# Attention steps of four heads, a free accumulator, and matmuls on constants while the first loads run

## The chip, the cores and the metric

The kernel runs on one core of a Trainium2 chip. The metric is the device time in microseconds, the median of several runs. TensorE (PE) does the matmuls, VectorE (DVE) and ScalarE (ACT) work on their operands and results, GpSimd (POOL) makes masks, and SyncE (SP) issues most of the loads.

## The reference, cut to what matters

Three mixers over a sequence of 256 tokens of 2048 features, each with its input and output projections in full precision:

- `hybrid_layer`: a convolution branch (gated input, 31 taps, layer norm) beside attention with 16 heads of 64 features, two shared keys and values, a window of 128 and a sink per head. Its output is projected, added to the input and normed.
- `_dsa_mixer`: an index of 16 heads of 64 features scores the earlier tokens and keeps the best 64 for each query (`k_top = min(256, S // 4)`); attention with 16 heads of 128 features in four groups of four, each group with one key and one value head, runs over the kept ones.
- `_stick_breaking_mixer`: 16 heads of 128 features with their own keys and values; the weights come from sums of log-sigmoids.

The second and third are each followed by a norm and a gate: `x = x + (p[i] @ w_ple[i]) * sigmoid(x @ w_ple_gate[i])`.

## The kernel before

**Projections.** Every large product is made of matmuls on operands split into two parts (`hi`, `lo`): three products stand for one in full precision. `gemm` (L315) keeps activations stationary and streams 512 weight columns (L324 to L326); `gemm_T` (L329) keeps 128 weight columns stationary: per k-tile and feature tile of 128 columns, one matmul of 512 columns on both parts of the activation (L336), one of 256 columns for the low part of the weight (L338). `granules` (L291) walks the weight in pieces of one, two or four k-tiles. `fetch` (L268) loads a piece, casts its high part on ACT (L277) and subtracts on DVE (L278), two pieces ahead; `plan` fixes the order of the weights.

**PSUM.** `acc` has two tiles of two banks for the projections, `aux` four banks that `bank` (L215) hands out for everything else: scores, transposes, weighed values. `gemm_T` takes one `acc` tile for each two feature tiles, so `gv0` (gate and value together, four feature tiles) takes both. `total` (L341) adds the two halves of a result: an ACT copy, then a DVE addition.

**Side work.** `Side` (L153) holds lanes of generators. After each weight piece `pump` lets every lane take a step, lanes "a" and "b" in turn. The scheduler then orders instructions by program order and by when it takes them to be ready; each engine runs its own queue in order.

- `conv` (L502) in lane "conv": 31 multiply-adds on DVE for each of eight channel tiles, three taps a step.
- `soften` (L534) for two heads: scores into a bank each, the row minimum of the negated scores on DVE, then a step with the exponentials and the scaling on ACT (or DVE), then a step with three transposes a head into a bank each and their copies. `attn1` (L624) calls it for head i of both key groups, one on partitions 0 to 63 and the other on 64 to 127, so its score matmuls use half the rows (L547, L548) and its weighing half the columns (L593, L594); these are in full precision. A record of the profile is one pass; a full-precision matmul has two.
- `index()` (L918): 16 heads, two a step (L926, L927), each with a relu on ACT (L929) that frees its bank and two DVE multiply-adds.
- `attn2` (L985): scores of 128 queries in full precision (L543) and of the others in three split matmuls (L545); weighing by `weigh_split` (L596), three split matmuls (L602) and a full-precision one of 128 columns (L603) a head.
- `attn3` (L1038): a step per head with three split matmuls (L1044) and a full-precision one (L1048) into a bank that stays in use until its exponential; then two steps of sums by triangular ones (L1062, L1063), then `weigh_split`.

The transposes of `kvT` into `v1` (L731) stand straight behind the projection `kv`.

## Time and profile before

| | |
|---|---|
| median of 3 runs | 1449.77 us (1449.68 to 1450.47) |
| the profiled execution | 1450.28 us, its span 1448.6 us |
| PE busy | 1432.4 us, 8076 matmul records |
| DVE, ACT busy | 1032.3 us, 802.9 us |
| HBM read | 262.53 MB, 183 GB/s |

The page gives each engine's busy time, then the span in 40 slices. A row of the timeline is a run of like instructions on one engine: start, time from the first start to the last end, engine, line, operation, shapes, count, and in brackets the idle time before it with what ended it. Matmuls overlap in these rows (their ends are modelled); what one costs is read from start to start.

### The profile page before, as it was taken

What the parts mean: (1) busy time and instruction counts of PE and PEld (TensorE: products, weight loads), DVE (VectorE), ACT (ScalarE), POOL (GpSimd) and SP (SyncE); (2) the same over time, 40 slices, a digit from 0 to 9 for tenths busy, and PEclk for the clock granted to TensorE, in tenths of its full rate; (3) what the DMA queues carried; (4) which work ended last, traced back from release to release, by engine and by line L of the source; (5) the groups of instructions that cost most, each with busy time, mean ns of one, the idle gap of its engine ahead of it and who ended that gap; (6) DMA issues with size and microseconds to landing.
All of it is one profiled execution on the core that took longest, in us unless ns stands there. A gap on an engine that the chain in (4) does not pass through costs nothing.

```text
span 1448.6 us, 21304 instructions
## 1 busy us (share of the span) xinstructions
PE 1432.4 (99%) x8076; PEld 1240.1 (86%) x8076; DVE 1032.3 (71%) x1588; ACT 802.9 (55%) x1199; POOL 23.1 (2%) x51
## 2 busy tenths in 40 slices
PE   7999999999999999999999999999999999999998
PEld 6888888888997888888898898888888888889888
DVE  6999989998679966766758655655555555575754
ACT  6445778475545556646544545655655656554442
POOL 0000000000000000000000000100100001000000
PEclk9999999999999999999999999999999999999999
DMA  9765445556375655454764555555555555586462
GB/s 300 273 202 176 153 139 173 186 186 230 92 238 160 204 162 173 148 186 152 260 201 148 184 178 187 162 176 188 169 179 175 175 176 167 185 266 218 128 219 75
DMA packets 79798, 266.01 MB, mean 184 GB/s; under 512 B 9408, under 2 KB 10048, under 8 KB 79696
## 3 DMA queue, kind: packets, MB, share of 16 engines
q1 hardware_dynamic: 79632, 264.63, 56.5%
q8 instruction: 63, 1.03, 0.3%
q14 instruction: 39, 0.32, 0.1%
q0 software_dynamic: 64, 0.03, 0.0%
HBM read 262.53 MB, written 2.10 MB: 183 GB/s over the span
## 4 chain that ended last, share of the span: by engine, by line
PE 93%; DVE 4%; DMA 1%; issue 1%; ACT 1%; DVEq 0%; SPq 0%
PE acc L336 31%; PE acc L338 15%; PE acc L324 14%; PE acc L326 14%; PE acc L325 14%; DVE wlo L278 1%; PE o L602 1%; PE pt L383 1%; PE pT L578 1%; PE o L603 0%; DVE u L448 0%; DVE u L509 0%; PE z L1044 0%; PE z L1062 0%; DMA raw<-in_w_in_a 0%
## 5 line engine op out<-in xcount | busy, mean ns | idle before, releaser
L278 DVE TENSOR_TENSOR wlo<-raw,whi 128x1024 fp32r<-128x1024 f32 (+3 forms) x475 | 563.2, 1190 | 309.0 <-ACT whi L277 304.6
L277 ACT CAST whi<-raw 128x1024 fp32r<-128x1024 f32 (+3 forms) x475 | 485.2, 1025 | 489.3 <-PE acc L336 220.4
L336 PE MATMUL acc<-u,whi 128*128 128x512 f32 x2016 | 637.2, 399 | 7.3 <-DVE u L377 5.6
L338 PEld LDWEIGHTS acc<-u,wlo 128*128 128x128 f32 x2016 | 377.0, 188 | 87.7
L338 PE MATMUL acc<-u,wlo 128*128 128x256 f32 x2016 | 394.9, 279 | 0.0
L324 PE MATMUL acc<-whi,u 128*128 128x512 f32 (+3 forms) x1004 | 359.0, 358 | 0.0
L325 PE MATMUL acc<-wlo,u 128*128 128x512 f32 (+3 forms) x1004 | 355.9, 354 | 0.8 <-DVE wlo L278 0.8
L326 PE MATMUL acc<-whi,u 128*128 128x512 f32 (+3 forms) x1004 | 355.6, 354 | 0.0
L336 PEld LDWEIGHTS acc<-u,whi 128*128 128x128 f32 x2016 | 309.3, 189 | 14.2 <-ACT whi L277 5.6
L326 PEld LDWEIGHTS acc<-whi,u 128*128 128x128 f32 x1004 | 189.7, 189 | 25.4 <-DVE u L377 0.4
L324 PEld LDWEIGHTS acc<-whi,u 128*128 128x128 f32 x1004 | 189.8, 189 | 25.0 <-issue 1.7
L325 PEld LDWEIGHTS acc<-wlo,u 128*128 128x128 f32 x1004 | 189.9, 189 | 24.3 <-DVE wlo L278 1.2
L509 DVE SCALAR_TENSOR_TENSOR u<-u,convw,u 128x255 f32<-128x255 f32 (+19 forms) x240 | 109.2, 465 | 3.9
L351 DVE TENSOR_TENSOR h<-acc,h 128x512 f32<-128x512 f32 x51 | 34.8, 684 | 4.8 <-ACT h L345 4.8
L376 ACT CAST u<-h 128x512 fp32r<-128x512 f32 (+1 forms) x32 | 18.0, 566 | 25.3 <-DVE h L615 17.5
L466 DVE TENSOR_TENSOR u<-u,h 128x1024 f32<-128x1024 f32 x24 | 28.5, 1219 | 3.4 <-DMA h<-in_ln_g 3.3
L377 DVE TENSOR_TENSOR u<-h,u 128x512 fp32r<-128x512 f32 (+1 forms) x32 | 19.7, 622 | 14.4 <-ACT u L376 14.1
L1034 POOL TENSOR_SCALAR_AFFINE_SELECT h<-h 128x256 f32<-128x256 f32 x32 | 18.1, 564 | 743.8 <-DVE h L1054 715.7
L558 ACT ACTIVATE u<-u,negm 128x128 f32<-128x128 f32 x64 | 28.4, 445 | 2.7 <-DVE negm L550 2.6
L345 ACT ACTIVATE h<-acc 128x512 f32<-128x512 f32 x42 | 24.9, 593 | 5.5 <-PE acc L338 4.0
L802 DVE TENSOR_TENSOR h<-h,u 128x512 f32<-128x512 f32 (+1 forms) x20 | 10.8, 582 | 20.8 <-ACT h L801 20.8
L277 ACT CAST u<-raw 128x1024 fp32r<-128x1024 f32 (+1 forms) x17 | 17.3, 1015 | 14.2 <-DMA raw<-in_w_ple 7.4
(197 smaller groups left out, 962.8 us busy)
## 6 DMA issues: line engine op xcount, KB each, us to landing
raw<-in_w_in_a SPq DMA_DIRECT2D x80, 512.0 KB, 3.6
raw<-in_w_in SPq DMA_DIRECT2D x76, 512.0 KB, 3.4
raw<-in_w_gate SPq DMA_DIRECT2D x64, 512.0 KB, 3.6
raw<-in_w_kv_b SPq DMA_DIRECT2D x64, 512.0 KB, 3.4
raw<-in_w_q_b SPq DMA_DIRECT2D x64, 512.0 KB, 3.3
raw<-in_w_out SPq DMA_DIRECT2D x32, 512.0 KB, 3.4
raw<-in_w_out_a SPq DMA_DIRECT2D x32, 512.0 KB, 4.3
raw<-in_w_out_b SPq DMA_DIRECT2D x32, 512.0 KB, 4.4
```

Of the source, the lines that this page charges most:

```text
L277: nc.scalar.copy(hi, raw)
L278: return hi, lo, nc.vector.tensor_tensor(lo, raw, hi.bitcast(F32), ALU.subtract)
L324: nc.tensor.matmul(o, ah, wh, start=first, stop=False)
L325: nc.tensor.matmul(o, ah, wl, start=False, stop=False)
L326: nc.tensor.matmul(o, al, wh, start=False, stop=last)
L336: nc.tensor.matmul(ps[f // 2][:, f % 2], wh[:, f * P:(f + 1) * P], both, start=first, stop=False)
L338: nc.tensor.matmul(ps[f // 2][:, f % 2, 0, :], wl[:, f * P:(f + 1) * P], ah, start=False, stop=last)
L345: nc.scalar.activation(t, ps[:, :, 1, :], AF.Copy, scale=scale)
L351: nc.vector.tensor_tensor(out_, ps[:, :, 0, :], t, ALU.add)
L466: nc.vector.tensor_tensor(self.z[c], self.z[c], r.unsqueeze(1).broadcast_to([P, 2, 512]), op)
L509: nc.vector.scalar_tensor_tensor(o[:, d:], h[:, :S - d], w, o[:, d:], ALU.mult, ALU.add)
L558: nc.scalar.activation(sc[:, i, cs], sc[:, i, cs], AF.Exp, bias=negm[:, i, tt:tt + 1], scale=-1.0, accum_out=den[:, i, tt:tt + 1],)
```

## The change

`WARM` matmuls on `ones_mean` into a bank that nobody reads stand right behind the constants. `gemm_T` takes one `acc` tile for its first two feature tiles and a bank of `aux` for each further one (only `gv0` has such), and `total` takes these as a list. The transposes into `v1` stand behind the projection of `q0`. `soften` takes four heads: four banks of scores, then per two heads the minima, the exponentials, and after twelve transposes the copies, each a step of its own; split heads issue all full-precision scores ahead of all split ones. `attn1` and `attn2` use it in one lane, "heads", which steps at every pump. `index()` issues four heads' matmuls at once. The second attention's values are split for both token tiles (`both_split`), its probabilities for the late queries too, and `weigh_shared` multiplies the late queries of two heads in one matmul of 256 columns, three in all, in place of two full-precision ones. `weigh_split`, now for the third attention alone, and `attn3` issue the split matmuls of both heads ahead of the full-precision ones.

```diff
+WARM = 9
...
+    idle = bank("idle")
+    for i in range(WARM):
+        nc.tensor.matmul(idle[:, 0:P], ones_mean, ones_mean, start=True, stop=True)
...
         nf = _cols(STREAMS[stream][key][0]) // P
-        ps = [acc.tile([P, 2, 2, S], F32, tag="acc", name=uid("acc")) for _ in range(nf // 2)]
+        two = acc.tile([P, 2, 2, S], F32, tag="acc", name=uid("acc"))
+        ps = [two[:, f] for f in range(2)]
+        ps += [bank("acc").rearrange("p (h s) -> p h s", h=2) for _ in range(2, nf)]
         for kt, first, last, wh, wl in granules(stream, key, events):
-            both, ah = act.both(kt), act(kt, slice(0, S))[0]
+            pair, ah = act.both(kt), act(kt, slice(0, S))[0]
             for f in range(nf):
-                nc.tensor.matmul(ps[f // 2][:, f % 2], wh[:, f * P:(f + 1) * P], both, start=first, stop=False)
+                nc.tensor.matmul(ps[f], wh[:, f * P:(f + 1) * P], pair, start=first, stop=False)
             for f in range(nf):
-                nc.tensor.matmul(ps[f // 2][:, f % 2, 0, :], wl[:, f * P:(f + 1) * P], ah, start=False, stop=last)
-        return ps
+                nc.tensor.matmul(ps[f][:, 0, :], wl[:, f * P:(f + 1) * P], ah, start=False, stop=last)
+        return [two, ps[2:]][:nf // 2]
...
+        if isinstance(ps, list):
+            for f, p in enumerate(ps):
+                nc.scalar.activation(t[:, f, :], p[:, 1, :], AF.Identity, bias=bias1[:, bias + f:bias + f + 1])
+                nc.vector.tensor_tensor(out_[:, f, :], p[:, 0, :], t[:, f, :], ALU.add)
+            return out_
...
     def soften(heads, mask, scale):
+        twos = (heads[:2], heads[2:])
+        split = heads[0][2] is None
+        sc = [unit((P, 2, 384)) for _ in twos]
...
+        ps = [bank("s", 384) for _ in heads]
+        for p, (q, k, h) in zip(ps, heads):
+            if split:
+                nc.tensor.matmul(p[:, 0:128], q.raw, k.raw, start=True, stop=False)
+            else:
+                nc.tensor.matmul(p[:, 0:128], q[:, 0:128], k[:, 0:128], start=True, stop=True)
+                nc.tensor.matmul(p[:, 128:384], q[:, 128:256], k, start=True, stop=True)
+        if split:
+            for p, (q, k, h) in zip(ps, heads):
                 for m, (a, b) in enumerate(((q.hi, k.hi), (q.hi, k.lo), (q.lo, k.hi))):
+                    nc.tensor.matmul(p[:, 128:384], a, b, start=False, stop=m == 2)
+        for j, two in enumerate(twos):
+            for i, (q, k, h) in enumerate(two):
+                for tt, cs in enumerate(QUERIES):
+                    nc.vector.tensor_tensor_reduce(
+                        sc[j][:, i, cs], ps[2 * j + i][:, cs], mask[:, cs], -scale,
+                        3e38 if split else nsink[:, h:h + 1], ALU.add, ALU.min, negm[j][:, i, tt:tt + 1],
+                    )
+            yield
...
+        pts = [bank("pT", 384) for _ in heads]
+        for i, pt in enumerate(pts):
+            for b in range(3):
+                nc.tensor.transpose(pt[:, b * P:(b + 1) * P], sc[i // 2][:, i % 2, b * P:(b + 1) * P], ident)
+        out_ = []
+        for j in range(2):
+            if split:
+                late, early = short((P, 2, 2, P), F32R), []
+                for i, pt in enumerate(pts[2 * j:2 * j + 2]):
+                    wp = short((P, 2, S), F32R)
+                    nc.scalar.copy(wp[:, 0, :], pt[:, 0:S])
+                    nc.vector.tensor_tensor(wp[:, 1, :], pt[:, 0:S], wp[:, 0, :].bitcast(F32), ALU.subtract)
+                    hi, lo = late[:, 0, i, :], late[:, 1, i, :]
+                    nc.scalar.copy(hi, pt[:, S:384])
+                    nc.vector.tensor_tensor(lo, pt[:, S:384], hi.bitcast(F32), ALU.subtract)
+                    early.append(wp)
+                out_.append((early, late))
             else:
+                pb = [short() for _ in range(2)]
+                for i in range(2):
+                    nc.scalar.copy(pb[i], pts[2 * j + i])
                 out_.append(pb)
+            if j == 0:
+                yield
...
         vv, vl = v
         for i, (h, (wp, late)) in enumerate(zip(heads, probs)):
-            cs = slice(h * P, (h + 1) * P)
-            for m, (a, b) in enumerate(((0, 0), (0, 1), (1, 0))):
-                nc.tensor.matmul(po[:, i, :], vv[:, a, cs], wp[:, b, :], start=i == 0 and m == 0, stop=False)
-            nc.tensor.matmul(po[:, i, P:S], vl[:, cs], late, start=False, stop=i == 1)
+            for m, (a, b) in enumerate(PARTS):
+                nc.tensor.matmul(
+                    po[:, i, :], vv[:, a, h * P:(h + 1) * P], wp[:, b, :], start=i == 0 and m == 0, stop=False
+                )
+        for i, (h, (wp, late)) in enumerate(zip(heads, probs)):
+            nc.tensor.matmul(po[:, i, P:S], vl[:, h * P:(h + 1) * P], late, start=False, stop=i == 1)
+    def weigh_shared(po, v, probs, h):
+        early, late = probs
+        for i, wp in enumerate(early):
+            for m, (a, b) in enumerate(PARTS):
+                nc.tensor.matmul(
+                    po[:, i, :], v[0][:, a, h * P:(h + 1) * P], wp[:, b, :], start=i == 0 and m == 0, stop=False
+                )
+        for m, (a, b) in enumerate(PARTS):
+            nc.tensor.matmul(po[:, :, P:S], v[1][:, a, h * P:(h + 1) * P], late[:, b], start=False, stop=m == 2)
...
+    def both_split(ps):
+        out_ = [unit((P, 2, 512), F32R) for _ in range(2)]
+        for vv, p in zip(out_, ps):
+            nc.scalar.copy(vv[:, 0, :], p)
+            nc.vector.tensor_tensor(vv[:, 1, :], p, vv[:, 0, :].bitcast(F32), ALU.subtract)
+        return out_
...
-    def attn1(i):
+    def attn1(j, f):
         rows = (slice(0, 64), slice(64, 128))
-        gen = soften([(qT[i // 4][r, i % 4, :], kvT[r, 0, :], 8 * j + i) for j, r in enumerate(rows)], mask1, 0.125)
+        ii = (2 * f, 2 * f + 1)
+        gen = soften(
+            [(qT[j][r, i, :], kvT[r, 0, :], 8 * g + 4 * j + i) for i in ii for g, r in enumerate(rows)], mask1, 0.125
+        )
         for probs in gen:
             yield
-        while i // 4 not in sagT:
-            yield
-        po = bank("o1", S)
-        for r, p in zip(rows, probs):
-            weigh(po[r, :], [v1[:, tt, r] for tt in range(2)], p)
-        gate_into(yact, 8 + i, 1, po.rearrange("p (k s) -> p k s", k=1), sagT[i // 4][:, i % 4:i % 4 + 1, :])
+        while j not in sagT:
+            yield
+        po = [bank("o1", S) for _ in ii]
+        for o, two in zip(po, probs):
+            for r, p in zip(rows, two):
+                weigh(o[r, :], [v1[:, tt, r] for tt in range(2)], p)
+        for o, i in zip(po, ii):
+            gate_into(yact, 8 + 4 * j + i, 1, o.rearrange("p (k s) -> p k s", k=1), sagT[j][:, i:i + 1, :])
         yield
...
     glu(3)
     projected("kv", kvT)
-    pt = transposes([kvT[:, 1, tt * P:(tt + 1) * P] for tt in range(2)])
-    nc.scalar.copy(v1, pt[:, :S].rearrange("p (k s) -> p k s", k=2))
     for j in range(2):
         for f, h in enumerate("xy"):
             projected(f"q{j}{h}", qT[j][:, 2 * f:2 * f + 2, :])
-        for i in range(4 * j, 4 * j + 4):
-            side.add(attn1(i), 1, "ab"[i % 2])
+        if j == 0:
+            pt = transposes([kvT[:, 1, tt * P:(tt + 1) * P] for tt in range(2)])
+            nc.scalar.copy(v1, pt[:, :S].rearrange("p (k s) -> p k s", k=2))
+        for f in range(2):
+            side.add(attn1(j, f), 1, "heads")
         sag = unit((P, 4, S))
         for f, h in enumerate("xy"):
             projected(f"ag{j}{h}", sag[:, 2 * f:2 * f + 2, :], AF.Silu)
...
-    side.drain("a")
-    side.drain("b")
+    side.drain("heads")
...
+        for h0 in range(0, 16, 4):
+            ps = [bank("ix", 384) for _ in range(4)]
+            for h, p in enumerate(ps, h0):
+                rows = slice(64 * (h % 2), 64 * (h % 2) + 64)
+                qh = qiT[h // 2 // 3][:, h // 2 % 3, :]
+                nc.tensor.matmul(p[:, 0:128], qh[rows, 0:128], kiT[rows, 0:128], start=True, stop=True)
+                nc.tensor.matmul(p[:, 128:384], qh[rows, 128:256], kiT[rows, :], start=True, stop=True)
+            for h, p in enumerate(ps, h0):
...
+                if h % 2:
+                    yield
...
     kT2 = Turned("k", slice(0, S))
-    v2 = split_values(gemm("w_in_a_2", "v", xact))
+    v2 = both_split(gemm("w_in_a_2", "v", xact))
     yact = Act()
     SCALE2 = 128.0 ** -0.5
-    def attn2(qT2, c, heads, sgT):
+    def attn2(qT2, c, sgT):
         while not selected:
             yield
-        gen = soften([(qT2.head(h), kT2.head(c), None) for h in heads], bias2, SCALE2)
+        gen = soften([(qT2.head(h), kT2.head(c), None) for h in range(4)], bias2, SCALE2)
         for probs in gen:
             yield
         while c not in sgT:
             yield
-        po = bank("o2").rearrange("p (k s) -> p k s", k=2)
-        weigh_split(po, v2, probs, (c, c))
-        gate_into(yact, 4 * c + heads[0], 2, po, sgT[c][:, heads[0]:heads[0] + 2, :])
-        yield
+        po = [bank("o2").rearrange("p (k s) -> p k s", k=2) for _ in range(2)]
+        for o, two in zip(po, probs):
+            weigh_shared(o, v2, two, c)
+        for j, o in enumerate(po):
+            gate_into(yact, 4 * c + 2 * j, 2, o, sgT[c][:, 2 * j:2 * j + 2, :])
+            yield
...
-        side.add(attn2(qT2, c, (0, 1), sgT), 1, "a")
-        side.add(attn2(qT2, c, (2, 3), sgT), 1, "b")
+        side.add(attn2(qT2, c, sgT), 1, "heads")
...
     def attn3(q, k, c, heads, v3, sgT):
         zs, ws = [], []
-        for h in heads:
-            zz = bank("z", 384)
+        banks = [bank("z", 384) for _ in heads]
+        for zz, h in zip(banks, heads):
             blocks = zz.rearrange("p (b q) -> p b q", b=3)
             for i, (ks, qs) in enumerate(((k.hi, q.hi), (k.hi, q.lo), (k.lo, q.hi))):
                 nc.tensor.matmul(
                     blocks[:, 0:3:2, :], ks[:, h, 0:128], qs[:, h, :].rearrange("p (b q) -> p b q", b=2),
                     start=i == 0, stop=False,
                 )
+        for zz, h in zip(banks, heads):
             nc.tensor.matmul(zz[:, 128:256], k.late[:, h, :], q.late[:, h, :], start=False, stop=True)
+        for zz in banks:
             e, sp = short(), short()
             sh, sl = short(dt=F32R), short(dt=F32R)
             nc.scalar.activation(e, zz, AF.Abs)
```

## Rows read from the trace of the kernel before

**Rows 1.** The page: busy times, and the granted clock in 40 slices.

```profile
PE 1432.4 (99%) x8076; PEld 1240.1 (86%) x8076; DVE 1032.3 (71%) x1588; ACT 802.9 (55%) x1199; POOL 23.1 (2%) x51
...
PEclk9999999999999999999999999999999999999999
```

**Rows 2.** Who waited for whom, PE: us in total, times, longest us.

```profile
PE acc L336 <- DVE u L377: 5.6, 1, 5.6
...
PE acc L325 <- DVE wlo L278: 0.8, 1, 0.8
```

**Rows 3.** Timeline, all engines, from 0 to 34 us.

```profile
5.59 2.04 PE L336 MATMUL acc<-u,whi 128*128 128x512 f32 x4 [5.59 <-DVE u L377]
...
10.80 1.09 PE L336 MATMUL acc<-u,whi 128*128 128x512 f32 x4
...
26.47 0.69 DVE L377 TENSOR_TENSOR u<-h,u 128x512 fp32r<-128x512 f32 x1 [1.98 <-ACT u L376]
...
27.64 1.09 PE L336 MATMUL acc<-u,whi 128*128 128x512 f32 x4
...
29.97 0.63 PE L338 MATMUL acc<-u,wlo 128*128 128x256 f32 x4
...
32.27 0.73 PE L336 MATMUL acc<-u,whi 128*128 128x512 f32 x2 [1.67 <-DVE h L351]
```

**Rows 4.** A stretch: length, busy us of each engine, clock, DMA share, GB/s.

```profile
16.00:20.00 4.00, 4.00 (x25) 3.51 (x24) 2.19 (x5) 2.53 (x5) 0.00 (x0) 1.00 0.99 319
```

**Rows 5.** Timeline of PE from 108 to 121 us.

```profile
115.48 0.41 PE L383 MATMUL pt<-ident,h 128*128 128x128 f32 x2 [1.65 <-DVE h L351]
```

**Rows 6.** Timeline of PE from 136.5 to 140 us, a score group of the first attention.

```profile
136.87 0.63 PE L336 MATMUL acc<-u,whi 128*128 128x512 f32 x2
137.34 0.39 PE L338 MATMUL acc<-u,wlo 128*128 128x256 f32 x2
...
139.09 0.40 PE L338 MATMUL acc<-u,wlo 128*128 128x256 f32 x2
```

**Rows 7.** Timeline of PE from 148 to 170 us, a weighing group of it.

```profile
163.09 0.39 PE L338 MATMUL acc<-u,wlo 128*128 128x256 f32 x2
...
164.79 0.39 PE L338 MATMUL acc<-u,wlo 128*128 128x256 f32 x2
```

**Rows 8.** The chain that ended last: start us, us, what.

```profile
151.00 0.66 PE pT L578 x6
```

**Rows 9.** Timeline of PE at two index groups.

```profile
443.24 0.39 PE L338 MATMUL acc<-u,wlo 128*128 128x256 f32 x2
...
444.76 0.39 PE L325 MATMUL acc<-wlo,u 128*128 128x512 f32 x1
...
455.01 0.50 PE L926 MATMUL ix<-kiT,u 64*128 64x128 f32 x4
```

**Rows 10.** Timeline of ACT from 430 to 470 us, the relu of head 11.

```profile
456.31 0.49 ACT L929 ACTIVATE h<-ix 128x384 f32<-128x384 f32 x1 [2.81 <-DVE h L877]
```

**Rows 11.** Timeline of PE from 498 to 532 us, second attention, scores and weighing.

```profile
503.07 0.38 PE L543 MATMUL s<-h,h 128*128 128x128 f32 x2
...
503.64 0.39 PE L543 MATMUL s<-h,h 128*128 128x128 f32 x2
...
522.99 0.39 PE L338 MATMUL acc<-u,wlo 128*128 128x256 f32 x2
...
524.83 0.40 PE L338 MATMUL acc<-u,wlo 128*128 128x256 f32 x2
```

**Rows 12.** Line L543: what its engine waited for, us, times.

```profile
  ACT h L974: 1.8, 4
```

**Rows 13.** A stretch with the convolution, columns as in rows 4.

```profile
80.00:120.00 40.00, 38.35 (x221) 33.20 (x220) 39.58 (x71) 17.57 (x22) 0.00 (x0) 1.00 0.60 194
```

**Rows 14.** Who waited for whom, ACT, from 120 to 280 us.

```profile
ACT whi L277 <- PE acc L336: 32.8, 24, 1.9
```

**Rows 15.** Line L1044: what its engine waited for, us, times.

```profile
  DVE u L1028: 1.2, 4
```

More of the change, by code (lines that the diff above doesn't have):

```diff
@@ L348, in total @@
                 nc.scalar.activation(t[:, f, :], ps[:, f, 1, :], AF.Identity, bias=bias1[:, bias + f:bias + f + 1])
-        out_ = t if out_ is None else out_
         if scale == 1.0:
@@ L564, in soften @@
-        if heads[0][2] is not None:
-            nc.vector.tensor_tensor(den, den, es, ALU.add)
-        nc.vector.reciprocal(den, den)
-        for i in range(n):
-            for tt, cs in enumerate(QUERIES):
-                if h is None:
-                    nc.vector.tensor_scalar(sc[:, i, cs], sc[:, i, cs], den[:, i, tt:tt + 1], None, ALU.mult)
-                else:
-                    nc.scalar.activation(sc[:, i, cs], sc[:, i, cs], AF.Copy, scale=den[:, i, tt:tt + 1])
-        yield
-        out_ = []
@@ L575, in soften @@
-        for i in range(n):
-            pt = bank("pT", 384)
-            for b in range(3):
-                nc.tensor.transpose(pt[:, b * P:(b + 1) * P], sc[:, i, b * P:(b + 1) * P], ident)
-            if h is None:
-                wp, late = short((P, 2, S), F32R), short((P, P))
-                nc.scalar.copy(wp[:, 0, :], pt[:, 0:S])
-                nc.vector.tensor_tensor(wp[:, 1, :], pt[:, 0:S], wp[:, 0, :].bitcast(F32), ALU.subtract)
-                nc.scalar.copy(late, pt[:, S:384])
-                out_.append((wp, late))
-            else:
-                pb = short()
-                nc.scalar.copy(pb, pt)
+        twos = (heads[:2], heads[2:])
@@ new lines, in soften @@
+        for j, two in enumerate(twos):
+            es = small.tile([P, 2, 2], F32, tag="es", name=uid("es"))
+            for i, (q, k, h) in enumerate(two):
+                for tt, cs in enumerate(QUERIES):
+                    nc.scalar.activation(
+                        sc[j][:, i, cs], sc[j][:, i, cs], AF.Exp, bias=negm[j][:, i, tt:tt + 1], scale=-1.0,
+                        accum_out=den[j][:, i, tt:tt + 1],
+                    )
+                if not split:
+                    nc.scalar.activation(es[:, i, :], negm[j][:, i, :], AF.Exp, bias=sink[:, h:h + 1])
+            if not split:
+                nc.vector.tensor_tensor(den[j], den[j], es, ALU.add)
+            nc.vector.reciprocal(den[j], den[j])
+            for i in range(2):
+                for tt, cs in enumerate(QUERIES):
+                    if split:
+                        nc.vector.tensor_scalar(sc[j][:, i, cs], sc[j][:, i, cs], den[j][:, i, tt:tt + 1], None, ALU.mult)
+                    else:
+                        nc.scalar.activation(sc[j][:, i, cs], sc[j][:, i, cs], AF.Copy, scale=den[j][:, i, tt:tt + 1])
+            yield
```

57 lines of the change are left out of this document (15 added, 42 removed).

## The prediction

> **What bounds the kernel now.** I read the page's busy times first, then PE's waits, then PE's timeline at the places that the change touches. PE is busy 99% of the span at full clock from its first slices on [rows 1]. Busy alone proves little, since matmuls overlap in the records; what proves it are the waits. In 1448.6 us PE waits 5.6 us for its first operands and 0.8 us for a split weight; the other two waits of note are 1.67 and 1.65 us [rows 2, 3, 5]. Everything else is start following start: two k-tiles of gv0, eight L336 of 512 columns and eight L338 of 256, take 2.80 us [rows 3], so a k-tile with two feature tiles takes 0.70: a pair of L336 0.47 [rows 6], a pair of L338 the other 0.235. So the time is the sum of what PE is given to do plus those few holes, and an edit counts by what it takes out of PE's stream or out of a hole, as long as ACT and DVE, which split each weight (L277, L278), keep up. In the stretch with the convolution DVE is busy 39.58 of 40 us [rows 13], so there this "as long as" is the question.
>
> My unit is the insertion: from the L338 pair before a foreign group to the next L338 pair, less the plain 0.70 us.
>
> **The change part by part.**
>
> *Warm-up.* Nine full-precision matmuls on ones_mean run while the first loads fly. Before, PE starts at 5.59 and its first two k-tiles of gv0 take until 10.80, that is 5.21 us; two later ones take 2.80 (27.64 to 29.97, plus the last four L338, 0.47) [rows 3]. At most 2.4 us are there to be had. But gv0 is fed by loads: the split of the last x pair ends at 27.16 and its k-tiles start at 27.64, so the end of gv0 can move by 0.48 at most unless that load comes sooner, and the DMA engines are at 0.99 [rows 3, 4]. Between 0 and 0.48 I take **0.25 us**. [...]
>
> *gv0's accumulators.* Two of four feature tiles go to the four-bank pool, so g1 finds a free accumulator. Before, gv0's last matmul ends at 30.44 and g1 starts at 32.27, released by the total at L351 [rows 3]. Gone: **1.83 us**. What is late next is g1's own split weight; the wait names the total alone, so the weight was there before it. Bounds 1.2 to 1.9, the lower if DVE, which then has 1.8 us less in hand, makes one late later.
>
> *Values of the first attention.* The two transposes of kvT that waited 1.65 us for a total [rows 5] move behind q0's two projections, 32 k-tiles or 22 us later; the wait goes whole, and the copy v1 is needed only by the first weighing, later still. **1.65 us**, bounds 1.2 to 1.65.
>
> *First attention, scores and weighing in fours.* A score group of two heads: L338 at 137.34, next L338 at 139.09, less 0.70: 1.05 us [rows 6]. What would it cost inside a longer group? A pass of 128 full-precision columns takes 0.11 us (six transposes in 0.66 us [rows 8]); a pair needs 128 and 256 columns in two passes each (its four records of a line are two heads times two passes, the heads side by side on 64 rows each), twice 0.11 and twice 0.22: 0.66 us. The 0.39 left over is entering and leaving the 64-row form. Eight groups become four: 4 x 0.39 = **1.56 us**. Weighing: 164.79 - 163.09 - 0.70 = 1.00 [rows 7], same columns, so 4 x 0.34 = **1.36 us**. Each lies between half of this (if entry costs again within the group, for which no row exists) and all. The probability transposes have no such overhead: 0.66 for six is six times 0.11, so twelve in a row gain nothing.
>
> *Index in fours.* The same form: 443.24 to 444.76 less an L338 pair (0.235) and one L324 (0.23) is 1.05 [rows 9], eight groups to four, 1.56 us. But four banks are the whole pool, and the last group of four takes its banks when head 11's relu is done. That relu runs 456.31 to 456.80 while PE was at heads 12 and 13 already at 455.01 [rows 9, 10]: 1.8 us of waiting where none was, since before it needed heads 8 and 9 alone. Between +1.56 and -1.8 (both ends of rows) I take **0**, because the stretch ends in PE's 0.8 us wait for a split weight [rows 2], which says that DVE sets its end.
>
> *Second attention.* Grouping full-precision before split scores: one head takes 0.57 us (503.07 to 503.64) [rows 11], and 2 x 0.11 plus 3 x 0.118 is 0.57, so a switch between the kinds costs next to nothing in this form. The first one waits for its operand, 1.8 us over the four chunks [rows 12]; the new order wants the same operand first. **0.2 us**, bounds 0 to 1.8. Shared values: two heads were 524.83 - 522.99 - 0.70 = 1.14 us [rows 11]; six split matmuls plus three shared ones of 256 columns are 9 x 0.118 = 1.06. Eight times 0.08: **0.65 us**, bounds 0.3 (if the output in two strips of 128 were slower) to 0.9. Added beside it are one more 512-column split of v, and per two heads two short ACT copies and DVE subtractions of 128 columns; they lie on DVE and ACT, busy 71% and 55% of the span [rows 1], and cost nothing while probabilities are ready a step ahead; if not, each is at most one such operation late.
>
> *Third attention.* Four z matmuls wait for the low half of q or k, 1.2 us together [rows 15]; grouping two heads lets PE take another head's ready matmul first. **0.4 us** of 0 to 1.2. The reordered weighing gains nothing by the switch price above: **0**.
>
> Sum: 0.25 + 1.83 + 1.65 + 1.56 + 1.36 + 0 + 0.2 + 0.65 + 0.4 = 7.9 us. The profiled execution took 1450.28 us (1448.6 of span); by it the new time is 1442.4. The median of the runs is 0.5 us lower, so **1441.9 us**. All lower ends together (with 0.8 + 0.7 for the two fours and -1.8 for the index) give 2.4 us or 1447.4; all upper ends, 12.4 us or 1437.4.
>
> **The rivals.**
>
> *ACT and DVE set the pace (0.13).* With DVE at 39.58 of 40 us, a PE that runs 5 us earlier through the convolution may only wait more for split weights, and everything saved before the index is given back; left are 0.2 + 0.65 + 0.4 plus a part of the rest, some 2 us: **1447.8**. For it: that DVE row. Against it: from 120 to 280 us ACT's cast of the next weight waits 24 times for PE to let a buffer go, 32.8 us in all [rows 14], so the helpers are held back by PE there and not the other way.
>
> *Banks become the bound (0.08, slower).* Steps of four ask for all four banks at once: 4 score and 4 transposing steps in the first attention, the same in the second, 4 in the index, 20 in all. Before, a step needed two, and its readers had a step more of time. If each waits for the last reader, PE loses what DVE or ACT is behind. The break-even is 7.9 / 20 = 0.4 us each; at 0.6 us, a third of the 1.8 us that the index row gives, the loss is 12 us: **1453.9**. Against it: between scores and transposes lie four steps, and only the index reuses its banks two steps later.
>
> [...] Worked from rows: a fall to the lower level at each of the 20 steps for one k-tile pair of the kind that took 5.21 instead of 2.80 us would cost some 48 us, near **1490**. This case's trace speaks against it, the clock row shows full speed across both holes of 1.7 us [rows 1, 3, 5]; I give it 0.01.
>
> *The warm-up pays in full (0.04).* If the loads come sooner once PE frees its buffers sooner, all 2.4 us of the slow opening return, 2.15 more than I count: **1439.7**. The DMA share of 0.99 speaks against it.
>
> [...]
>
> That the change does not do what it says is possible for the warm-up alone (the clock may rise no sooner); that costs 0.25.
>
> **How the numbers follow.** Forecast 0.74 at 1441.9 (own range 1437.4 to 1447.4), pace 0.13 at 1447.8, banks 0.08, clock 0.01, full warm-up 0.04. The range 1436.9 to 1447.4 takes in the bounds of the unknown costs and the full warm-up's likeliest time. A measurement here can tell about 0.2% or 2.9 us from no change, so faster means under 1446.9: 0.74 + 0.04 and a little of the pace case, 0.79; same 0.12; slower 0.09.
>
> **What would show it.** Right: no wait of PE for L351 in the first 130 us; half as many 64-row score groups, each near 1.7 us for four heads; z and weighing groups as priced. Wrong: new rows of PE waiting for ACT or DVE at a score, index or transposing group (banks), or for the split weight L278 between 40 and 300 us (pace); a full clock well before 10 us with gv0 ending near 28 (warm-up).

## The result and the profile after

The changed kernel takes 1441.94 us (median of 6 runs, 1440.59 to 1443.18) against 1449.72 us (1448.77 to 1453.32): a ratio of 0.9942, 95% interval 0.993 to 0.9955, so 6.5 to 10.1 us less. The forecast was 1441.9 us. The profiled execution took 1443.18 us, its span 1441.5; before it was 1448.6, so the two traces differ by 7.1 us, and it is these that the terms are measured in.

From the page of the changed kernel:

```profile
span 1441.5 us, 21329 instructions
PE 1431.0 (99%) x8086; PEld 1245.7 (86%) x8086; DVE 1033.7 (72%) x1606; ACT 798.4 (55%) x1195; POOL 24.3 (2%) x51
```

What PE waits for in it (us in total, times, longest):

```profile
PE acc L330 <- DVE wlo L283: 1.5, 2, 0.9
PE acc L346 <- DVE u L392: 1.2, 3, 0.8
PE idle L229 <- DVE halfpi L910: 1.2, 1, 1.2
```

The kernel is bound as before [rows 1]: PE is busy 99% of the span. The two waits for a total (L351 before, now L366) are gone [rows 3, 5]. One wait has doubled, that of L330 for a split weight (0.8 us before [rows 2]). L346 waits for a split of x three times instead of once, though for less time in all, since the warm-up now fills most of the wait for the first one. L346 and L348 are the old L336 and L338, L329 to L331 the old L324 to L326.

PE's timeline of the changed kernel shows the terms one by one: the warm-up and gv0, gv0's end, the transposes of kvT, a group of scores, a group of weighing, the index's two waits, and the shared values.

```profile
1.15 4.21 PE L229 MATMUL idle<-ones_mean 128*128 128x128 f32 x18 [1.15 <-DVE halfpi L910]
6.19 2.04 PE L346 MATMUL acc<-u,whi 128*128 128x512 f32 x4 [0.83 <-DVE u L392]
...
11.10 1.08 PE L346 MATMUL acc<-u,whi 128*128 128x512 f32 x4
...
14.21 1.20 PE L346 MATMUL acc<-u,whi 128*128 128x512 f32 x4 [0.17 <-DVE u L392]
...
17.45 1.20 PE L346 MATMUL acc<-u,whi 128*128 128x512 f32 x4 [0.16 <-DVE u L392]
...
31.11 0.64 PE L348 MATMUL acc<-u,wlo 128*128 128x256 f32 x4
31.58 0.63 PE L346 MATMUL acc<-u,whi 128*128 128x512 f32 x2
...
132.06 0.40 PE L348 MATMUL acc<-u,wlo 128*128 128x256 f32 x2
132.29 0.38 PE L398 MATMUL pt<-ident,h 128*128 128x128 f32 x2
...
132.97 0.40 PE L348 MATMUL acc<-u,wlo 128*128 128x256 f32 x2
...
135.06 0.40 PE L348 MATMUL acc<-u,wlo 128*128 128x256 f32 x2
135.39 0.50 PE L561 MATMUL s<-h,u 64*128 64x128 f32 x4
135.71 0.61 PE L562 MATMUL s<-h,u 64*128 64x256 f32 x4
136.15 0.49 PE L561 MATMUL s<-h,u 64*128 64x128 f32 x4
136.37 0.70 PE L562 MATMUL s<-h,u 64*128 64x256 f32 x4
...
137.58 0.40 PE L348 MATMUL acc<-u,wlo 128*128 128x256 f32 x2
...
160.51 0.39 PE L348 MATMUL acc<-u,wlo 128*128 128x256 f32 x2
...
162.90 0.40 PE L348 MATMUL acc<-u,wlo 128*128 128x256 f32 x2
...
447.72 0.50 PE L330 MATMUL acc<-wlo,u 128*128 128x512 f32 x1 [0.65 <-DVE wlo L283]
453.50 0.50 PE L330 MATMUL acc<-wlo,u 128*128 128x512 f32 x1 [0.90 <-DVE wlo L283]
...
518.12 0.40 PE L348 MATMUL acc<-u,wlo 128*128 128x256 f32 x2
...
520.99 0.39 PE L348 MATMUL acc<-u,wlo 128*128 128x256 f32 x2
```

Read as the prediction read it, from L348 to the next L348 less 0.70: the transposes cost 0.21 us, four heads' scores 1.82 (two cost 1.05 before [rows 6]), four heads' weighing 1.69 (two cost 1.00 [rows 7]), two pairs' values 2.17 (one cost 1.14 [rows 11]). g1's first L346 stands at 31.58, right behind gv0's last L348.

Over all groups of each kind, in us of PE's time saved:

| term | forecast | the two traces | where it is read |
|---|---|---|---|
| warm-up | 0.25 | -1.14 | gv0 ends at 31.58, before at 30.44 |
| gv0's accumulators | 1.83 | 1.83 | g1 starts at once |
| transposes of kvT | 1.65 | 1.84 | 2.06 before, 0.21 to 0.23 after |
| first attention, scores | 1.56 | 1.22 | 8 x 1.05 to 1.06, then 4 x 1.80 to 1.83 |
| first attention, weighing | 1.36 | 1.24 | 8 x 0.99 to 1.02, then 4 x 1.70 |
| index | 0 | 0 | 9.5 in both, waits for split weights included |
| second attention, scores | 0.2 | 0.79 | 10.54, then 9.75, waits included |
| second attention, values | 0.65 | 0.70 | 8 x 1.17, then 4 x 2.16 |
| third attention, z | 0.4 | 0.5 | 10.26, then 9.76 |
| sum | 7.9 | 7.0 | |

A new wait for a split weight at 73.6 us costs 0.4. It stands in all six traces with a warm-up (this one and those of experiments 1 to 4 and 7), and at 0 to 0.2 us in the eight without, so it goes with the warm-up. The projections' 7248 matmul records are the same in both traces and come in the same order; followed along their starts, the saving is -1.14 us at gv0's end, 2.3 ahead of the first attention, 4.8 behind it, 4.75 behind the index, 6.3 behind the second attention and 7.1 at the end. So the 0.5 us that the table and the wait leave open are 0.1 behind gv0, 0.1 in the second attention and 0.2 in the third (0.7 there in all); the rest is rounding.

### The profile page after: what moved, and what is told of

The parts are those of the page before. It is cut to its first block, busy times and chain, and to the rows that moved or that the text cites. A ratio compares the mean times of both kernels' runs of the same rounds, so it can differ in the third digit from the quotient of the medians.

```text
span 1441.5 us, 21329 instructions
## 1 busy us (share of the span) xinstructions
PE 1431.0 (99%) x8086; PEld 1245.7 (86%) x8086; DVE 1033.7 (72%) x1606; ACT 798.4 (55%) x1195; POOL 24.3 (2%) x51
## 4 chain that ended last, share of the span: by engine, by line
PE 96%; DVE 2%; ACT 1%; DMA 0%; issue 0%; DVEq 0%
PE acc L346 32%; PE acc L348 16%; PE acc L329 14%; PE acc L331 14%; PE acc L330 14%; PE pt L398 1%; PE pT L598 1%; DVE u L463 0%; PE z L1125 0%; PE z L1105 0%; PE o L633 0%; PE o L644 0%; DVE wlo L283 0%; PE s L566 0%; PE o L623 0%; DMA h<-in_xT 0%
## 5 line engine op out<-in xcount | busy, mean ns | idle before, releaser
L346 PE MATMUL acc<-u,whi 128*128 128x512 f32 x2016 | 636.3, 398 | 1.2 <-DVE u L392 1.2
L348 PEld LDWEIGHTS acc<-u,wlo 128*128 128x128 f32 x2016 | 377.4, 188 | 87.9 <-DVE wlo L283 0.5
L348 PE MATMUL acc<-u,wlo 128*128 128x256 f32 x2016 | 395.0, 279 | 0.1
L329 PE MATMUL acc<-whi,u 128*128 128x512 f32 (+3 forms) x1004 | 358.3, 357 | 0.0
L330 PE MATMUL acc<-wlo,u 128*128 128x512 f32 (+3 forms) x1004 | 356.5, 355 | 1.5 <-DVE wlo L283 1.5
L331 PE MATMUL acc<-whi,u 128*128 128x512 f32 (+3 forms) x1004 | 355.9, 355 | 0.0
L346 PEld LDWEIGHTS acc<-u,whi 128*128 128x128 f32 x2016 | 309.7, 190 | 6.2 <-issue 2.5
L330 PEld LDWEIGHTS acc<-wlo,u 128*128 128x128 f32 x1004 | 190.1, 189 | 25.8 <-DVE wlo L283 2.3
L331 PEld LDWEIGHTS acc<-whi,u 128*128 128x128 f32 x1004 | 189.9, 189 | 25.1 <-DVE u L392 0.4
L329 PEld LDWEIGHTS acc<-whi,u 128*128 128x128 f32 x1004 | 189.9, 189 | 24.3 <-issue 0.7
L524 DVE SCALAR_TENSOR_TENSOR u<-u,convw,u 128x255 f32<-128x255 f32 (+22 forms) x240 | 108.4, 471 | 3.1
L366 DVE TENSOR_TENSOR h<-acc,h 128x512 f32<-128x512 f32 x50 | 34.3, 686 | 2.2 <-ACT h L364 2.2
L392 DVE TENSOR_TENSOR u<-h,u 128x512 fp32r<-128x512 f32 (+1 forms) x32 | 19.9, 621 | 10.0 <-ACT u L391 9.7
```

The lines of the kernel that those rows point to most:

```text
L329: nc.tensor.matmul(o, ah, wh, start=first, stop=False)
L330: nc.tensor.matmul(o, ah, wl, start=False, stop=False)
L331: nc.tensor.matmul(o, al, wh, start=False, stop=last)
L346: nc.tensor.matmul(ps[f], wh[:, f * P:(f + 1) * P], pair, start=first, stop=False)
L348: nc.tensor.matmul(ps[f][:, 0, :], wl[:, f * P:(f + 1) * P], ah, start=False, stop=last)
L366: nc.vector.tensor_tensor(out_, ps[:, :, 0, :], t, ALU.add)
```

## The experiments

Each kernel was timed beside the kernel before on the same chip (four chips in all; there the kernel before took 1450.88 to 1451.81 us by its medians). So ratios compare across groups, microseconds only within one. The interval of a ratio is about 0.0013 to either side, 1.9 us.

**1. The warm-up taken out, made longer, and the other edits undone or moved (one chip).**

```
-WARM = 9
+WARM = 0        (e1_nowarm)
+WARM = 12       (e2_warm12)
```

> The changed kernel without its nine matmuls on constants. Theory: in the changed kernel's trace the granted clock rose 10.65 us after the span's start, in the one before at 10.74, so the matmuls did not lift it; then this kernel stays at 1441.9 within 0.5 us, its clock rises near 10.7 us and PE still takes some 5.2 us for the first two k-tiles. Rival 1, they bring what I counted: 0.25 us slower. Rival 2, they hold up the first load (the first x pair was cast at 4.70 in place of 4.10 us): here the cast is back at 4.1, and the time 0.6 us or more below 1441.9.

> Twelve matmuls on constants in place of nine, so that PE has no idle time before the first projection (there were 0.83 us). If that gap kept the clock low, the clock rises before 9 us, the first two k-tiles take under 4.5 us, and gv0 ends up to 1 us earlier: 1441 us. If the matmuls do not lift it, the clock rises near 10.7 us again and the first projection starts at about 6.7 in place of 6.2 us: 1441.9 to 1442.4 us.

Without warm-up: 1439.6 us (1439.45 to 1442.2), ratio 0.9926 [0.9914, 0.9939]. With twelve: 1441.22 us (1441.07 to 1442.86), 0.9936 [0.9924, 0.9949]. So the warm-up brought nothing, and the run without it was the shortest of all. The intervals overlap with each other and with that of the changed kernel; that the kernel is faster without warm-up is not shown.

**2. First attention back in twos, the rest as changed** (its scores, probabilities and weighing by the old loop).

```
-    def attn1(j, f):
+    def attn1(i):
...
+        gen = soften2([(qT[i // 4][r, i % 4, :], kvT[r, 0, :], 8 * j + i) for j, r in enumerate(rows)], mask1, 0.125)
```

> The changed kernel with the first attention back in steps of two heads in two lanes. Theory (PE's stream sets the time): eight score groups of 1.06 us in place of four of 1.81, eight weighing groups of 1.00 in place of four of 1.70: 2.5 us slower, 1444.4 us. Rival (DVE and ACT set the pace through the convolution): the same matmul groups come back, but the time stays within 0.8 us of 1441.9.

1444.11 us (1443.14 to 1445.1), ratio 0.9955 [0.9942, 0.9969]; 2.9 us above the twelve-matmul run, the nearest to it of the same chip with a warm-up, and none of the five runs of the one falls among those of the other. Against the changed kernel, on another chip, the intervals overlap. One score group of two heads in it:

```profile
133.89 0.40 PE L348 MATMUL acc<-u,wlo 128*128 128x256 f32 x2
...
135.64 0.40 PE L348 MATMUL acc<-u,wlo 128*128 128x256 f32 x2
```

From 133.89 to 135.64 less 0.70 is 1.05, the price of before. Eight score groups and eight of weighing cost 16.5 us of PE here, four and four 14.0 in the changed kernel: 2.5 us. The term is in the price of the groups, and by the medians it reaches the end. The traced spans alone wouldn't show it (1441.4 us here, 1441.5 in the changed kernel): this trace ends gv0 1.2 us sooner and lacks one wait at the index. Had banks been the bound, twos would have been shorter.

**3. The affine steps of the second block's first norm moved behind v** (they stand on DVE between the weight splits of the index).

```
-    side.add(ln.affine(), 1, "late")        (at the index's start)
+    side.add(ln.affine(), 1, "late")        (behind v2)
```

> The changed kernel with the affine part of the first norm on DVE (24 operations of 1.22 us in three norms, 8 of them here) started behind the second attention's values in place of beside the index. Theory (DVE sets the pace at the index): PE's two waits there (0.81 and 1.18 us beyond the plain step) shrink to under 0.5 together: 1440.2 us. Rival (the four banks set it): relus on ACT still come late, the waits stay, under 0.4 us of difference. A loss of up to 1 us is possible where these operations then meet the second attention.

1445.39 us (1444.69 to 1447.6), ratio 0.9964 [0.9952, 0.9977]. The index's two waits are gone, and the time is longer all the same. PE's timeline, and then a stretch with its granted clock (the column behind POOL's):

```profile
494.34 0.63 PE L346 MATMUL acc<-u,whi 128*128 128x512 f32 x2
498.83 1.18 PE L559 MATMUL s<-h,h 128*128 128x128 f32 x4 [3.86 <-ACT h L1033]
499.66 1.63 PE L566 MATMUL s<-u,u 128*128 128x256 f32 x6
```

```profile
499.00:502.00 3.00, 3.00 (x14) 2.90 (x15) 2.72 (x12) 3.00 (x12) 0.00 (x0) 0.50 0.16 44
```

The steps now fall on the first scores of the second attention. PE waits 3.86 us for ACT's copy there, and behind that wait its granted clock is 0.50 for some 3 us: ten score matmuls that take 1.15 us elsewhere take 2.2.

**4. The order of ACT's casts, with and without warm-up (one chip, with 5 and 6).** In the changed kernel the third and fourth cast of x stand behind one weight cast more than in the kernel before and in the run without warm-up: the matmuls of the warm-up made the planner move them. These two kernels keep casts of gv0 in the order of the program, the first with the warm-up and for the pairs shown, the second without it and for all later ones too.

```
-        nc.scalar.copy(hi, raw)
+        cast = nc.scalar.copy(hi, raw)
+        if p[1] == "gv0" and p[2] in (6, 7, 8):
+            tc.keep_in_program_order(cast)
...
-        xact.put(kt, 2, raw)
+        xact.put(kt, 2, raw, kt in (4, 6))      (and there: keep_in_program_order)
```

> The changed kernel with its nine warm-up matmuls, but ACT casts the third and the fourth pair of x ahead of the weight cast that stands before each in the changed kernel (the order of the kernel before). Theory 'queue order': the warm-up matmuls cost nothing themselves; they made the planner put one weight cast, which must wait for PE to let a buffer go, ahead of the third and the fourth x cast. Then PE's waits for an x split (0.33 and 0.10 us, before the rows at 14.21 and 17.45) go, the end of gv0 moves from 31.6 to 29 to 30 us, and the time is 1438.5 to 1440.5 us. Rival 'warm-up itself': the nine matmuls hold back the start; then gv0 still ends at 30.4 to 31.6 and the time is 1441 to 1442.5 us.

> The changed kernel without warm-up matmuls, with the same order of ACT's first 26 casts as the run with the casts put back. Beside that run it shows the warm-up by itself. Theory 'queue order': equal to the run without warm-up, 1439.6 us within 1, gv0 ends at 29 to 30 us, and 0 to 2 us more than the run that keeps the warm-up, since the clock rises some us later. Rival 'warm-up itself': 1439.6 too, but 1.5 us or more below the run that keeps the warm-up.

1440.54 us (0.9929 [0.9916, 0.9941]) and 1440.38 us (0.9928 [0.9915, 0.9942]): the same. gv0's first and third k-tile, and g1's start, with the warm-up and then without:

```profile
5.49 1.43 PE L348 MATMUL acc<-u,whi 128*128 128x512 f32 x4
...
8.78 1.20 PE L348 MATMUL acc<-u,whi 128*128 128x512 f32 x4
...
29.07 0.63 PE L348 MATMUL acc<-u,whi 128*128 128x512 f32 x2
```

```profile
5.77 2.04 PE L348 MATMUL acc<-u,whi 128*128 128x512 f32 x4 [5.77 <-DVE u L396]
...
10.49 1.08 PE L348 MATMUL acc<-u,whi 128*128 128x512 f32 x4
...
30.13 0.63 PE L348 MATMUL acc<-u,whi 128*128 128x512 f32 x2
```

In this pair the warm-up did what it is for, gv0 ended 1.06 us sooner, and the spans are 1438.8 us both. PE keeps about 1 us of it until the first index group, at 432 us. DVE loses it before: from 417 us on, with a weight split queued behind, it waits for rows of ln_g, and by 431 us it stands at the same time in both (first kernel, then the second):

```profile
417.23 1.23 DVE L485 TENSOR_TENSOR u<-u,h 128x1024 f32<-128x1024 f32 x1 [0.77 <-DMA h<-in_ln_g]
...
421.49 1.23 DVE L485 TENSOR_TENSOR u<-u,h 128x1024 f32<-128x1024 f32 x1 [0.76 <-DMA h<-in_ln_g]
...
431.27 0.69 DVE L1035 TENSOR_TENSOR u<-h,u 128x512 fp32r<-128x512 f32 x1 [0.69 <-ACT u L1034]
```

```profile
417.85 1.23 DVE L485 TENSOR_TENSOR u<-u,h 128x1024 f32<-128x1024 f32 x1 [0.42 <-DMA h<-in_ln_g]
...
431.24 0.69 DVE L1035 TENSOR_TENSOR u<-h,u 128x512 fp32r<-128x512 f32 x1 [0.69 <-ACT u L1034]
```

My theory of the order is not borne out: gv0 did end sooner (29.07 for 31.58), but with the order of before, the kernel with the warm-up is not shown to differ in time from the changed one (0.9929 and 0.9942, overlapping intervals), a later kernel with the same order (7, below) again waits 1.2 us for x, and the three other kernels with the warm-up and the changed order (1 to 3) end gv0 at 30.13 to 30.45. Over all fourteen traces gv0 ends at 29.07, 29.99, 30.13, 30.39, 30.45 and 31.58 us with a warm-up, and at 29.55 to 30.96 without (eight traces, the middle two 30.14 and 30.32). The third k-tile starts at 8.78 to 9.71 in five of the six with a warm-up, at 9.90 to 11.04 without. The opening is quicker and the end is not. What takes the lead away shows in PE's waits: without a warm-up none is listed for a split of x after the first operand, with one there are one to three, 0.3 to 1.4 us in all. In the first kernel here ACT's casts of x wait for their loads four times, 3.1 us together, so loads have a part in it; how much the order of ACT's queue adds was not separated.

**5. gv0's accumulators alone, in the kernel before** (the diff's gemm_T and total, nothing else).

> The kernel before with gv0's second pair of feature tiles in the four-bank pool, and nothing else of the change. Theory (the forecast's term): g1 starts as gv0 ends, the wait of 1.67 us for the total is gone, 1.8 to 1.9 us less than the kernel before. Rival: g1's split weight is late next, or ACT and DVE give the time back in the convolution: within 0.7 us of the kernel before.

1448.0 us (1446.15 to 1448.61), ratio 0.9976 [0.9966, 0.9986]. The wait for the total is gone, and in its trace two later waits show what became of the time:

```profile
PE acc L325 <- DVE wlo L278: 1.9, 1, 1.9
PE pt L393 <- DVE h L361: 0.8, 1, 0.8
```

The index's wait for a split weight grew from 0.8 to 1.9, and that of the kvT transposes shrank from 1.65 to 0.8; the span is 1.7 us shorter. By the medians it is 3.0 us; the kernel before spreads from 1449.0 to 1453.34 on this chip, and the interval, 2.0 to 4.9 us, has the expected 1.8 to 1.9 just outside. Where the rest comes from is open, and so is whether the index's longer wait follows from the earlier start of g1: in experiment 6 that wait is gone altogether.

**6. The transposes of kvT moved, alone, in the kernel before** (the two lines of the diff behind q0's projections).

> The kernel before with the two transposes of kvT and the copy of v1 moved behind q0's two projections, and nothing else. Theory (the forecast's term): the wait of 1.65 us goes whole, the two transposes cost 0.23 us where they stand, 1.7 to 1.8 us less than the kernel before. Rival: the copy of v1 collides with the first score groups and PE waits there, or the time is given back in the convolution: within 0.7 us of the kernel before.

1448.46 us (1446.86 to 1450.91), ratio 0.9982 [0.9973, 0.9991], 1.3 to 3.9 us less, as priced. No wait stands at the transposes of kvT or at the first weighing. The span is 3.4 us shorter: 1.8 of it are the transposes, 0.8 the index's wait for a split weight, which is gone, and 0.45 an earlier end of gv0.

**7. The index in twos, and three ways to relieve DVE there.** The first three are without warm-up, on one chip; the last is the kernel with the warm-up and the casts in order, on another.

```
-                    nc.vector.tensor_tensor(self.z[c], ...)
+                    nc.gpsimd.tensor_tensor(self.z[c], ...)     (e9_pool)

-    side.add(ln.affine(), 1, "late")
+    side.add(ln.affine(), 1, "a")       (every other granule; e10_half)

-        for h0 in range(0, 16, 4):
-            ps = [bank("ix", 384) for _ in range(4)]
+        for h0 in range(0, 16, 2):
+            ps = [bank("ix", 384) for _ in range(2)]     (e11_ix2)

-        nc.sync.dma_start(            (a row of ln_g or ln_b)
+        nc.gpsimd.dma_start(          (e12_rows)
```

> The changed kernel without warm-up, with the normalised rows' affine steps (multiply by ln_g, add ln_b) on POOL in place of DVE. Theory 'DVE sets the index': these steps stand in DVE's queue between the weight splits of the index stretch and wait there for rows that are still loading; with them gone PE's wait for a split weight at the index (1.0 us in the run without warm-up) goes and the time falls to 1438 to 1439 us. Rival 'POOL disturbs DVE': DVE's splits grow longer beside POOL's work, the wait stays, 1439.5 us or more.

> The changed kernel without warm-up, with the affine steps of the second block's first norm issued at every other granule in place of every one, so that they reach beyond the index. Theory 'DVE sets the index': half of the 8 steps of 1.22 us leave the stretch before the last index group, PE's wait there (1.0 us) goes, 1438.3 to 1439.2 us. Rival: the steps only move the lack of DVE to the selection and to the first scores of the second attention, which wait instead; 1439.5 to 1441 us.

> The changed kernel without warm-up, with the index in steps of two heads again. Theory (the forecast's term of 0): eight groups cost PE 1.0 us more than four, and the wait for a split weight shrinks by as much, since DVE sets the end; within 0.5 us of 1439.6. Rival 'entry price': PE sets the end, 1440.3 to 1441 us. Rival 'banks': steps of four made the wait, 1438.5 us or less.

> The run with the x casts put back (warm-up kept, 1440.5 us), with the rows ln_g and ln_b of the affine steps loaded through POOL's queue in place of SP's, where they stand behind weight loads that wait for buffers; nothing else. Theory 'late rows': in the first of these runs DVE waited 0.77 and 0.76 us for ln_g rows (417.23 and 421.49 us) with weight splits queued behind, and that swallowed the 1.06 us by which gv0 ended sooner than without warm-up (29.07 against 30.13 us); issued earlier, both waits go, PE's wait for a split weight at the index (0.8 us) falls to 0.3 or less, and the time is 1439 to 1439.8 us. Rival 'buffers': the rows' buffers come free no sooner than SP issued them, the waits stay, 1440.2 to 1441 us. Rival 'queue cost': POOL's loads cost DVE more than they give, over 1441 us.

*Index in twos:* 1441.86 us, ratio 0.9934 [0.9921, 0.9946], beside 0.9926 [0.9914, 0.9939] for fours without warm-up: no difference that is shown, though the 1.2 us between the ratios leaves room for the rival's 1.0 us as well, and 1439.6 within 0.5 was missed. Its trace speaks for the theory. The groups cost 8.5 us as in the kernel before, the wait for the split weight (0.8 us in fours) is gone, and the first scores of the second attention wait 0.7 us that they didn't. *Half rate:* 1442.15 us, 0.9934 [0.9921, 0.9948], no gain as the rival said; the index's wait is gone, and others stand in its place. The waits of both, twos first:

```profile
PE s L559 <- ACT h L1034: 0.7, 1, 0.7
```

```profile
PE s L559 <- ACT h L1034: 1.2, 1, 1.2
PE acc L348 <- DVE wlo L283: 1.0, 2, 0.5
```

In the kernel without warm-up DVE is busy 19.2 to 19.9 of each 20 us from 440 to 500, so what it is spared at one place it lacks at the next. *Rows by another queue:* 1440.95 us, 0.9933 [0.9919, 0.9946]. The waits at 417 and 421 us went, one of 0.44 us for a later ln_g row came, the last index step on DVE began at 456.5 us as in both kernels of 4, and PE's wait for the split weight stayed (0.9 us). So the late rows were not the bound of DVE here. But in this run gv0 ended only 0.14 us before the second kernel of 4, so it had no lead for them to swallow, and what becomes of one is not settled by it.

*Affine steps on POOL* (the 24 of all three norms): 1461.37 us, ratio 1.0068 [1.0056, 1.0081], some 20 us worse than on DVE. DVE's index step L995 (smallest, middle and largest duration, ns, of 30), without warm-up and then with the steps on POOL; and the same kernel's steps on POOL (from 420 to 460 us) and two of PE's waits:

```profile
L995 DVE SCALAR_TENSOR_TENSOR h<-h,wi,h x30: 343/414/486, 433.0 to 455.5; 128x128 f32<-128x128 f32 x15, 128x256 f32<-128x256 f32 x15
```

```profile
L995 DVE SCALAR_TENSOR_TENSOR h<-h,wi,h x30: 340/474/2650, 436.3 to 465.2; 128x128 f32<-128x128 f32 x15, 128x256 f32<-128x256 f32 x15
```

```profile
L481 POOL TENSOR_TENSOR u<-u,h 128x1024 f32<-128x1024 f32 x8 | 24.9, 3124 | 98.1 <-DMA h<-in_ln_g 97.0 <-DMA h<-in_ln_b 0.9
```

```profile
PE ix L985 <- ACT h L989: 5.6, 3, 2.2
PE pt L398 <- DVE u L861: 4.5, 2, 4.3
```

The waits are not all of it. In or right behind such waits PE's granted clock falls to 0.50 three times, from 455.4 to 462.2 us, from 803.5 to 810.4 and from 1373.6 to 1377.0 (its mean over the span is 0.993, in the run without warm-up 0.999); a stretch of the first fall, columns as in rows 4:

```profile
456.00:462.00 6.00, 5.61 (x14) 4.09 (x15) 6.00 (x13) 4.68 (x9) 0.00 (x0) 0.50 0.09 15
```

Against the run without warm-up (experiment 1) the traced span is 23.2 us longer: PE's waits behind gv0 make up some 12 us more, gv0's end 1.4, and the 17 us at half the clock, with PE busy for about 15 of them, an estimated 7 to 8.

## Why the prediction was right, and where it was not

The median is nearer to the forecast than the terms deserve, and that part is luck; the profiled execution, in which they are measured, took 1443.18 us where 1442.4 was its forecast. The terms sized too high (warm-up by 1.39, scores 0.34, weighing 0.12) and those too low (second attention 0.64, transposes 0.19, z 0.1) leave 0.9, and the wait at 73.6 us, which no term had, nearly cancels against what the table's groups miss.

- **What bounds the kernel:** right. PE without holes sets the time, and the price per insertion carried over: undoing the first attention's part alone cost 2.9 us by the medians, 2.5 by its groups.
- **Warm-up:** the reasoning held in kind, neither the value nor the bounds did. That matmuls on constants quicken the opening at all was an assumption of mine that no row of before shows; it stands in five of the six traces that have them (third k-tile at 8.78 to 9.71 us, without them at 9.90 to 11.04), and not in the profiled execution. Once PE is ahead, late splits of x take the lead away, in fourteen traces with no visible gain at gv0's end. In the profiled execution PE waited 0.83 us between the warm-up and its first operand, the first k-tiles then took their old slow time (third k-tile at 11.10, before at 10.80), and gv0 ended 1.14 us later than before. The own range of the term, 0 to 0.48, left out a loss, and a gain beyond 0.48 too: the traces with a warm-up run from 29.07 to 31.58, before it was 30.44. Full clock from the first slices on, as I read it in the row of the clock, is not what that row can show (last section).
- **gv0's accumulators and the transposes:** right to 0.2 us. When the first was done alone, the index's wait was 1.1 us longer in its trace, which may be the "pace" rival in small and may be chance.
- **First attention in fours:** right in kind, too high in size. I took entering the 64-row form as paid once per group and nothing inside. Four heads cost 1.81 us where 1.32 + 0.39 = 1.71 was the price: 0.1 us more, and whether they are paid between the second and third head was not shown. Of weighing, 0.04.
- **Index:** 0 forecast, 0 found in this trace, and in the way given. PE's groups became some 1.1 us cheaper, and PE waits that much more for split weights. One trace doesn't carry it, though: the same 200 projection records around the index (from 414.6 to 464.3 us in the changed kernel) take 48.4 to 50.5 us in seven traces with fours and the affine steps in their old place, and 48.6 to 50.8 in four with twos. The loss of 1.8 us through banks, the other bound, didn't come: no wait for ACT's relu stands in the trace of the changed kernel. It does stand, with 0.3 us, in the first kernel of experiment 4, and with 5.6 us in the kernel with POOL, where DVE was late.
- **Second attention, order:** the largest error in a term that held its sign, 0.2 against 0.79. A plain group costs the same as before, 1.15 to 1.18 us for two heads; what fell is the wait for ACT's copy, 1.8 us over four chunks [rows 12], to 0.5 once. I had said that the new order wants the same operand first. What the traces show is another thing: before, the scores of four heads stood together; now they stand in two groups of two heads, 4 us apart, the first of them earlier in PE's stream by some 26 projection records, which may be why PE waits less for their operands. That this is the cause was not tried. The first head's row before, and the two groups' in the changed kernel:

```profile
501.76 0.49 PE L543 MATMUL s<-h,h 128*128 128x128 f32 x2
```

```profile
492.06 0.60 PE L559 MATMUL s<-h,h 128*128 128x128 f32 x4
...
496.02 0.71 PE L559 MATMUL s<-h,h 128*128 128x128 f32 x4
```

- **Shared values and z:** right within 0.1 by their groups; along the projections' starts the third attention gave 0.7 for 0.4, still inside its bounds.
- **Rivals:** *banks* is out for the changed kernel; no new wait for a bank stands in its trace. *Pace* has one of its signs there, the 0.4 us at 73.6 us, and it is true in part of one stretch, from 417 to 500 us: the 1.06 us of the warm-up in experiment 4 ended there, and the index's own 1.1. It is no fixed ceiling. The run without warm-up of experiment 1 enters that stretch as early as the first kernel of experiment 4 (the same projection matmul at 412.2 and 412.1 us) and leaves it 1.1 us sooner (460.6 and 461.7); what decides there is open. *The clock:* a fall at each of the 20 steps, the case given 0.01, is shown by no run. In the changed kernel the granted clock reads 1.00 up to its last microsecond. In experiment 3 it fell to 0.50 after a wait of 3.86 us for a copy. In the kernel with POOL it fell to 0.50 in the last of three waits for banks of the index (5.6 us together), and twice more at waits for DVE: there the clock did fall at a wait for banks, but for banks held by a late DVE.

## What to carry to other kernels

Price an insertion by what it displaces in the bounding engine's stream, and price it inside a group as well as at its edges. A gain ahead of a stretch where a second engine is full (here DVE, over 19 of 20 us) may not arrive whole; look for such stretches downstream before adding the terms up, and don't settle a term of 1 us there by one trace. In the runs here, moving a helper's work out of such a stretch moved the wait (to the first scores of the second attention, 3.86 us in experiment 3 and 1.2 us at half rate in 7); none found an engine and a place that were really free.

## What the runs showed of the hardware

- Some DVE steps were longer beside POOL's. With POOL's tensor_tensor (3.1 us each) in the index, single DVE steps took up to 2.65 us in place of 0.41 (L995) and 2.1 and 2.8 in place of 0.69 (L934), where one POOL step takes 3.1. Why was not tried.
- The clock column reads 0.50 in mid-kernel, from 499 to 502 us in experiment 3, after PE had waited 3.86 us. At the start it reads 1.00: in the changed kernel from 8 to 10 us (the row below), while four L346 take 2.04 us from 6.19 on and 1.08 from 11.10 on. The trace's own record of the clock begins at 10.65 us, with 1.00, and the column reads 1.00 ahead of it. So the start has to be read from durations; that the slow k-tiles there ran at a lower clock is an estimate from them and is not shown by the record.
- The first k-tiles behind the same nine matmuls didn't run equally fast in every execution. In the changed kernel the nine took 4.21 us, PE then waited 0.83 us, and four L346 took 2.04 us in the first k-tile and 1.90 in the second. In the first kernel of experiment 4 the nine took 4.21 us too, with 0.12 us (5.37 to 5.49) to the first operand, and the four took 1.43 us and then 1.08; in the kernel with rows by another queue, after 4.21 and 0.39 us, 1.58 and then 1.08. Two kernels with gaps of 0.36 and 0.78 us started fast as well, with 1.17 and 1.16 us, but there the nine matmuls took 3.97 and 3.61 us. That the gap of 0.83 us made the start slow is a guess from one trace: its first two k-tiles took 4.9 us, and without a warm-up they took anything from 4.3 to 5.3 in the eight traces.

The stretch from 8 to 10 us of the changed kernel, columns as in rows 4:

```profile
8.00:10.00 2.00, 2.00 (x8) 1.77 (x7) 1.91 (x3) 1.78 (x4) 0.00 (x0) 1.00 1.02 371
```
